# A decoder layer on one core: row scaling moved behind the up product, two beta products shifted, transposes placed later in a planned order

## The chip, the cores and the metric

One core of one Trainium2 chip runs the whole program. Its engines are TensorE (PE in the profile; PEld is its weight load), VectorE (DVE), ScalarE (ACT), GpSimd (POOL) and SyncE (SP), whose queue issues most DMAs. The metric is the device time of one execution in microseconds (us); smaller is better.

## The reference, cut to what matters

Sequence 512, model width 1024, one layer, all in float32. The parts that the change touches are the first projections and the gated MLP:

```
u = rmsnorm(h, g_mix);  proj = u @ w_in            # split into q, k, v, gates, beta and decay inputs (16 columns)
ro = retention(rotary(rq), rotary(rk), rv)          # 8 heads
do = gated_delta(l2norm(cq), l2norm(ck), cv, g, beta)  # 8 heads, chunks of 128, triangular solves
merged = sigmoid(gate_r) * (silu(rgate)*ro @ w_ret_br) + sigmoid(gate_d) * (do*silu(dz) @ w_dn_br)
h = h + merged @ w_o
u2 = (h * rsqrt(mean(h*h) + EPS)) * g_ffn           # one factor for each of the 512 rows
up = causal_dwconv(u2 @ w_up, ffn_conv_w) + ffn_conv_b   # 3 taps along the sequence
a, b = split(up);  h = h + (silu(a) * b) @ w_down
out = rmsnorm(h, g_final)
```

The factor of a row of h can be applied to u2, or to the product u2 @ w_up before the convolution: both give the same numbers up to rounding.

## The kernel before, in words

Each float32 operand of a large product is split in a high part (ACT casts it, `whi`, `ghi`, `u2hi`) and a rest (DVE subtracts, `wlo`, `glo`, `u2lo`), and a product is three matmuls, high by high, high by rest, rest by high (`mm3`, line 387). Weights come in blocks of 128x1024 through `wraw` and are split by the task `weights` (line 351); four split blocks fit (`WB`). The larger square products use seven block products instead of eight (`product`, line 449). Small products and transposes run in plain float32; a transpose is a matmul against the identity `cst`, four at a time (`transpose4`, line 544).

The order of the instructions on PE, ACT, DVE and POOL is the order in which the Python program issues them. A small planner makes it: `Order` (line 98). The long stream of large products is written out in sequence and moves a planned clock on. Everything else is a task, a generator, that waits in a heap until its planned time; `poll` (line 132), called after every three matmuls, lets the tasks run whose time has come. When a task yields, it is put back for the planned end of what it issued, `self.done`, plus 0.3 us, plus what it yields: `yield PW` with `PW = 0.6` (line 282) ahead of a transpose says how much later than the data's planned end the transposes are put into PE's stream. `issue` (line 114) notes the planned end of one instruction; `done` is that of the instruction issued last, also where an earlier one on another engine ends later. The SP queue is not among the engines whose order is set so (line 1795): the framework orders it itself.

The stages, in PE's order:

- Start: 11 warming matmuls, then `first_blocks` (line 1257). For each of the eight k tiles of x, which arrive by DMA and are split as `ghi`, `glo`, it issues three matmuls into `pk`, three into `pq`, and two into `pba` (the 16 beta and decay columns, weights `ba_w`, split by `ba_split`, line 666). The row sums of squares for the first norm go through `pss`.
- Fronts of the delta heads (`k_front`, `q_front`, `v_front`, lines 845 to 940), among products `pk`, `pq`, `pv`, with transposes `pkt`, `pqt`, `pvt`. Between the first four heads and the last four come the retention rows (`pr`), whose rotated rows are transposed (`prqT`, `prkT`, lines 1134 to 1150). `solve` and `scan` (lines 942 to 1078) do the triangular solves and the recurrence (`pm`, `psc`); `scan_end` (line 1080) normalizes a head's rows `vtok` and transposes them (`pot`). Retention's own products are `prs`, `pkv`, `pro`, `proT`.
- Gates (`pz`) and four square products (`py`); at the end of the last, `m_out` (line 1413) transposes the merged rows (`pmt`).
- The product with w_o (`po`) in the order of `OUT_ORDER`. `o_into` (line 1513) adds a result into h (`h`, DVE). When both halves of 128 rows are done it squares them (`junk`, ACT), makes the row factor `rr` (DVE, then a power on POOL, `rsqrt`), multiplies the rows by it into `hs` (one half on ACT, one on DVE), and `u2_out` transposes `hs` into `pt`. `u2_split` makes `u2hi` and `u2lo` of it, with g_ffn as the scale.
- Up product: 44 blocks, `pa` and `pb` in turn. `ffn_conv` (line 1574) reads the bank: ACT makes `acc` from tap 2 and the bias, DVE adds taps 1 and 0 (two multiply-adds of 512 columns). Silu, the product `r`, and sums for the down product follow. POOL meanwhile issues DMAs for sums of w_down's quarters, each after a tiny instruction `tock` that reads `tick` from ACT (`pace`, line 333).
- Down product (`pd`). `into` (line 1659) adds, squares, and at the end scales the two halves of 128 rows, `o` on ACT and `g` on DVE, and sends both out.

Of the kernel before, what the change touches and what calls it, by code (L numbers as in the profile page):

```python
# [11 lines left out]
F32 = mybir.dt.float32  # L12
F32R = mybir.dt.float32r
AF = mybir.ActivationFunctionType
ALU = mybir.AluOpType
# [82 lines left out]
class Order:  # L98
# [15 lines left out]
    def issue(self, engine, us, banks=()):  # L114

        at = self.clock if self.now is None else self.now
        at = max(at, self.free.get(engine, 0.0))
        for b in banks:
            at = max([at, *(t + self.HOP for e, t in self.banks.get(b, {}).items() if e != engine)])
        self.done = self.free[engine] = at + us  # L120
        for b in banks:
            self.banks.setdefault(b, {})[engine] = self.done

    def product(self, us):
        self.clock += us
# [6 lines left out]
    def poll(self):  # L132
        while self.tasks and self.tasks[0][0] <= self.clock:
            at, _, gen = heapq.heappop(self.tasks)
            self.now, self.done = at, None
            try:
                more = next(gen) or 0.0
                at = (at if self.done is None else self.done + self.HOP) + more
                self.n += 1
                heapq.heappush(self.tasks, (at, self.n, gen))  # L140
            except StopIteration:
                pass
            self.now = None

    def hold(self, cond):
        while not cond():
            self.clock = max(self.clock, self.tasks[0][0])
            self.poll()
# [89 lines left out]
def body(nc, tc, ctx, io):  # L238
# [26 lines left out]
    def s4(name, n=4, bufs=16):  # L265
        return mini.tile([P, n], F32, name=name, tag=f"n{n}", bufs=bufs)
# [259 lines left out]
    def row_scale(ssq, out):  # L526
        r = s4("rs", 1)
        vec.scalar_tensor_tensor(r, ssq[:, :1], EPS, ssq[:, 1:], ALU.add, ALU.add)
        yield
        rsqrt(out, r)  # L530
# [364 lines left out]
    def q_front(hd, ps):  # L895
        h = hd["h"]
        gb = row_decay(h) if "G" in have else None
        qT = hd["qT"] = yield from conv_silu(ps, h, f"q{h}")
        yield PW
        pqt = transpose4(qT, "pqt")  # L900
        yield
        ssq = s4("ssqq")
        junk = S("junk")
        for n in range(NT):
            act.activation(junk[:, ck(n)], pqt[:, ck(n)], AF.Square, accum_out=ssq[:, n:n + 1])
        yield
        vec.tensor_scalar(ssq, ssq, EPS, None, ALU.add)
        rq = s4("rq")
        yield
        rsqrt(rq, ssq)  # L910
        yield
        rqs = hd["rqs"] = mini.tile([P, 4], F32, name="rqs", tag="rqs", bufs=10)
        vec.tensor_scalar(rqs, rq, DK_SCALE, None, ALU.mult)
        while "k" not in hd["got"]:
            yield 0.3
        if gb is None:
            gb = row_decay(h)
        pqk = PS("pqk")
        for n in range(NT):
            pe.matmul(pqk[:, ck(n)], hd["kT"][:, ck(n)], qT[:, ck(n)], start=True, stop=True)  # L920
        yield
        hd["attn"] = em.pop(h)
        vec.tensor_tensor(hd["attn"], pqk, hd["attn"], ALU.mult)
        yield 1.5
        vec.tensor_tensor(qT, qT, gb, ALU.mult)
        hd["got"].add("q")

    def v_front(hd, ps):
        vT = yield from conv_silu(ps, 16 + hd["h"], f"v{hd['h']}")
        while "k" not in hd["got"]:  # L930
            yield 0.3
        yield PW
        pvt = transpose4(vT, "pvt")
        yield
        hd["vtok"] = S(f"vtok{hd['h']}")
        for n in range(NT):
            act.activation(hd["vtok"][:, ck(n)], pvt[:, ck(n)], AF.Identity, scale=hd["c1"][:, n:n + 1])
        hd["got"].add("v")
# [141 lines left out]
    def scan_end(hd, o, ssqo):  # L1080
        h = hd["h"]
        ms = s4("mso")
        vec.tensor_scalar(ms, ssqo, 1.0 / P, EPS, ALU.mult, ALU.add)
        r = s4("ro")
        yield
        rsqrt(r, ms)
        yield
        vec.tensor_tensor(v3(o), v3(o), bc(r), ALU.mult)
        hd["got"].add("o")
        yield PW  # L1090
        pt = transpose4(o, "pot")
        yield
        d = S(f"doT{h}")
        act.activation(d, pt, AF.Identity, scale=prm[:, P_DG:P_DG + 1])
        doT[h] = d
# [37 lines left out]

    def rq_front(t, _, ps):
        x = rotary(ps, t, "qrot")
        yield PW
        pt = transpose4(x, "prqT")
        yield
        q = S(f"rqT{t}")
        vec.tensor_tensor(q, pt, qdec, ALU.mult)  # L1140
        rqT[t] = v3(q)

    def rk_front(t, _, ps):
        x = rotary(ps, t, f"krot{t}")
        yield PW
        pt = transpose4(x, "prkT")
        yield
        k = S(f"rkT{t}")
        act.copy(k, pt)
        rkT[t], krot[t] = v3(k), v3(x)  # L1150
# [103 lines left out]

    pba = PS("pba")

    def first_blocks():

        pss = [PS(n) for n in ("pk", "pq")]
        ws = [tuple(v3(a, KT) for a in w) for w in first_w]  # L1260
        for k in range(KT):
            hold(lambda: k in g_ready)
            for i, ps in enumerate(pss):
                hold(lambda: (i, k // 4) in first_ready)
                mm3(ps, ws[i][0][:, k], ws[i][1][:, k], ghi[k], glo[k], k == 0, k == KT - 1)
                poll()
            hold(lambda: "ba" in first_ready)
            for j, x in enumerate(gx):
                pe.matmul(pba[:32], ba_w[:, k], x[k], start=(k + j == 0), stop=(k + j == KT))
            poll()  # L1270
        for i in range(2):
            spawn(weights(), 0.1 + 8.0 * i)
        spawn(decays(pba), 0.2)
        return pss
# [136 lines left out]
        o_opnd[name, t] = hi, lo  # L1411

    def m_out(t, i, r):
        yield 0.2
        pt = transpose4(r, "pmt")
        yield
        name, half = f"B{i + 1}{t // 2 + 1}", t % 2
        m = o_raw[name, half] = S(f"mr{t}{i}")
        act.copy(m, pt)
        yield  # L1420
        if name != "B12":
            spawn(o_split(name, half, m))
        if name == "B12":
            t3 = S("mt3")
            vec.tensor_tensor(t3, o_raw["B22", half], m, ALU.subtract)
            t2 = o_raw["T2", half] = S("mt2")
            vec.scalar_tensor_tensor(t2, t3, -1.0, o_raw["B11", half], ALU.mult, ALU.subtract)
            spawn(o_split("T2", half, t2), 0.2)
            yield 0.5
            t1 = S("mt1")  # L1430
            vec.tensor_tensor(t1, o_raw["B11", half], m, ALU.subtract)
            spawn(o_split("T1", half, t1), 0.2)
            spawn(o_split("T3", half, t3), 0.2)
        elif name == "B21":
            while o_now[0] < 3:
                yield 0.5
            t4 = S("mt4")
            vec.scalar_tensor_tensor(t4, o_raw["T2", half], -1.0, m, ALU.mult, ALU.subtract)
            spawn(o_split("T4", half, t4), 0.2)
# [68 lines left out]

    u2hi = [S(f"u2hi{k}", F32R) for k in range(KT)]
    u2lo = [S(f"u2lo{k}", F32R) for k in range(KT)]  # L1510
    ssqs = [s4("ssq1", 2) for _ in range(NT)]

    def o_into(t, i, ps, op, last=False):

        vec.tensor_tensor(h1[t][i], h1[t][i], ps, op)
        yield
        if not last:
            return
        junk = S("junk")
        act.activation(junk, h1[t][i], AF.Square, scale=1.0 / 32.0, accum_out=ssqs[t][:, i:i + 1])  # L1520
        if i == 0:
            return
        yield
        rr = s4("rr", 1)
        yield from row_scale(ssqs[t], rr)
        yield
        for i2 in range(2):
            xs = S("hs")
            if i2:
                vec.tensor_scalar(xs, h1[t][i2], rr, None, ALU.mult)  # L1530
            else:
                act.activation(xs, h1[t][i2], AF.Identity, scale=rr)
            spawn(u2_out(t, i2, xs), 0.6 * (i2 + 1))

    u2_ready = set()

# [35 lines left out]


    def ffn_conv(ps, ci):
        w = prm[:, P_FW + 3 * ci:P_FW + 3 * ci + 3]
        acc = S2("acc")
        act.activation(acc, ps, AF.Identity, scale=w[:, 2:3], bias=prm[:, P_FB + ci:P_FB + ci + 1])
        yield
        for j in (1, 0):
            s = 2 - j  # L1580
            vec.scalar_tensor_tensor(acc[:, s:], ps[:, :T - s], w[:, j:j + 1], acc[:, s:], ALU.mult, ALU.add)
        yield
        return acc
# [75 lines left out]
    def into(t, i, ps, op, c=slice(0, T), last=False):  # L1659
# [26 lines left out]
        o = hg[t, 1 - i]  # L1686
        act.activation(o, o, AF.Identity, scale=rr)
        vec.tensor_scalar(g, g, rr, None, ALU.mult)
        for k in (1 - i, i):
            sp.dma_start(ov[t, :, ck(k, T)], hg[t, k])  # L1690

    done = [0] * NT
# [106 lines left out]
```

## Time and profile before

| what | value |
|---|---|
| median of 3 runs | 981.6 us (980.06 to 982.82) |
| profiled execution, own time | 980.2 us |
| span from first to last instruction | 978.3 us |
| outside the span | 1.9 us |
| mean granted TensorE clock | 0.999 |
| PE busy | 963.4 us, 98% |
| DVE busy | 748.2 us, 76% |
| ACT busy | 529.1 us, 54% |
| POOL busy | 165.1 us, 17% |

A row of the timeline gives start, duration, engine, line, operation, output<-inputs, shape, and in brackets the engine's idle time before it and who ended it. Matmuls overlap in the profile: what counts is the distance from one start to the next. A float32 matmul stands as two records.

### The profile page before, as it was taken

Reading aid. Unit: us, or ns where it says so; the run is one execution under the profiler, and the core shown is the slowest. Engines: PE = TensorE matmul, PEld = TensorE weight load, DVE = VectorE, ACT = ScalarE, POOL = GpSimd, SP = SyncE. Lnnn points to the kernel's source line nnn. Section 1 sums busy time; section 2 is a strip of 40 time slices with the busy share of each in tenths; the row PEclk is TensorE's granted clock in tenths of the full one; section 3 lists DMA queues with packets and bytes.
Section 4 is the critical chain, followed back from the end, with each engine's and each line's share of the span. In section 5 each row is a group of like instructions: output and inputs, shape, how many; then the busy total and the mean of one; then the engine's idle time right before and its main releaser. Section 6 shows DMA issues by size and latency. Waiting matters only on the chain.

```text
span 978.3 us, 14091 instructions
## 1 busy us (share of the span) xinstructions
PE 963.4 (98%) x5133; PEld 804.6 (82%) x5133; DVE 748.2 (76%) x1359; ACT 529.1 (54%) x1110; POOL 165.1 (17%) x209
## 2 busy tenths in 40 slices
PE   8999999999999999999999999899999999999997
PEld 6888888788888888978888887788888888888886
DVE  6888898567888898585899799865555676688785
ACT  6598222256955323586686646854344434356663
POOL 0121322224344020132000000221122221000001
PEclk9999999999999999999999999999999999999999
DMA  8244569958797695579976855666579998346663
GB/s 277 83 126 143 168 197 215 275 143 214 214 210 215 182 229 147 144 207 270 256 229 197 281 154 160 208 211 217 193 204 213 227 201 195 91 143 191 192 202 118
DMA packets 82949, 189.27 MB, mean 193 GB/s; under 512 B 22912, under 2 KB 31680, under 8 KB 82880
## 3 DMA queue, kind: packets, MB, share of 16 engines
q1 hardware_dynamic: 55360, 123.36, 39.4%
q0 software_dynamic: 27520, 65.02, 29.9%
q8 instruction: 40, 0.66, 0.3%
q14 instruction: 29, 0.24, 0.1%
HBM read 185.17 MB, written 68.19 MB: 259 GB/s over the span
## 4 chain that ended last, share of the span: by engine, by line
PE 85%; DVE 6%; ACT 4%; DMA 2%; issue 2%; POOL 0%; SPq 0%; POOLq 0%; DVEq 0%; ACTq 0%
PE pb L230 12%; PE pa L230 12%; PE py L230 12%; PE pd L230 10%; PE pz L230 9%; PE pr L230 9%; PE pq L230 3%; PE pv L230 3%; PE psc L230 3%; PE pk L230 3%; DVE wlo L200 2%; PE po L230 2%; PE pro L230 1%; ACT whi L200 1%; PE pm L230 1%
## 5 line engine op out<-in xcount | busy, mean ns | idle before, releaser
L200 ACT CAST whi<-wraw 128x1024 fp32r<-128x1024 f32 (+1 forms) x214 | 219.9, 1029 | 184.9 <-PE pr L230 54.2
L200 DVE TENSOR_TENSOR wlo<-wraw,whi 128x1024 fp32r<-128x1024 f32 (+1 forms) x214 | 255.3, 1194 | 63.7 <-ACT whi L200 63.1
L200 POOL TENSOR_SCALAR tock<-tick 128x1 f32<-128x1 f32 x72 | 34.0, 472 | 399.6 <-ACT tick L200 399.6
L200 DVE SCALAR_TENSOR_TENSOR acc<-pb,prm,acc 128x511 f32<-128x511 f32 (+1 forms) x44 | 33.0, 749 | 57.0 <-ACT acc L200 56.2
L230 PE MATMUL pa<-u2lo,whi 128*128 128x512 f32 (+1 forms) x192 | 71.4, 372 | 0.0
L230 PE MATMUL pa<-u2hi,whi 128*128 128x512 f32 (+1 forms) x192 | 71.4, 372 | 0.0
L230 PE MATMUL pa<-u2hi,wlo 128*128 128x512 f32 (+1 forms) x192 | 71.3, 371 | 0.0
L230 PE MATMUL pb<-u2hi,whi 128*128 128x512 f32 (+1 forms) x184 | 70.0, 380 | 0.0
L230 PE MATMUL pb<-u2lo,whi 128*128 128x512 f32 (+1 forms) x184 | 69.9, 380 | 0.0
L230 PE MATMUL pb<-u2hi,wlo 128*128 128x512 f32 (+1 forms) x184 | 69.9, 380 | 0.0
L230 PE MATMUL py<-whi,oh 128*128 128x512 f32 x160 | 62.9, 393 | 0.0
L230 PE MATMUL py<-wlo,oh 128*128 128x512 f32 x160 | 62.3, 390 | 0.0
L230 PE MATMUL py<-whi,ol 128*128 128x512 f32 x160 | 62.3, 389 | 0.0
L230 PE MATMUL pd<-whi,T 128*128 128x512 f32 (+1 forms) x198 | 55.3, 366 | 0.0
L230 PE MATMUL pz<-ghi,whi 128*128 128x512 f32 x128 | 51.4, 402 | 0.0
L230 PE MATMUL pr<-whi,ghi 128*128 128x512 f32 x128 | 51.1, 399 | 0.0
L230 PE MATMUL pr<-whi,glo 128*128 128x512 f32 x128 | 50.0, 390 | 0.0
L230 PE MATMUL pz<-ghi,wlo 128*128 128x512 f32 x128 | 49.9, 390 | 0.0
L230 PE MATMUL pz<-glo,whi 128*128 128x512 f32 x128 | 49.9, 390 | 0.0
L230 PE MATMUL pr<-wlo,ghi 128*128 128x512 f32 x128 | 49.9, 390 | 0.0
L200 DVE SCALAR_TENSOR_TENSOR acc<-pa,prm,acc 128x511 f32<-128x511 f32 (+1 forms) x44 | 33.0, 749 | 19.0 <-ACT acc L200 18.2
L200 ACT ACTIVATE acc<-pb,prm 128x512 f32<-128x512 f32 x22 | 17.2, 780 | 48.5 <-PE pb L230 48.5
(331 smaller groups left out, 2416.2 us busy)
## 6 DMA issues: line engine op xcount, KB each, us to landing
wraw<-w SPq DMA_DIRECT2D x98, 512.0 KB, 4.8
s<-wm POOLq DMA_DIRECT2D x30, 1024.0 KB, 8.2
wraw<-s SPq DMA_DIRECT2D x60, 512.0 KB, 3.8
s<-wd POOLq DMA_DIRECT2D x24, 704.0 KB, 5.5
wraw<-wm SPq DMA_DIRECT2D x30, 512.0 KB, 4.5
s<-s POOLq DMA_DIRECT2D x10, 1024.0 KB, 11.8
wraw<-wd SPq DMA_DIRECT2D x15, 512.0 KB, 3.6
s<-s POOLq DMA_DIRECT2D x8, 704.0 KB, 9.4
```

The lines of the kernel that those rows point to most:

```text
L200: return f(out, *args, **kw)
L230: self.engine.matmul(out, lhsT, rhs, start=start, stop=stop, **kw)
```

## The change

Seven edits in one file:

- `Order.issue`: `done` becomes the latest planned end of all that a task issued since it last yielded, and not that of its last instruction. Every task that issues on two engines between yields can so come back later; this alone shifts places all over the program.
- Transposes are offered later: `q_front`, `v_front`, `rq_front` and `rk_front` yield 1.5 in place of `PW` (0.6); `scan_end` of heads 4 to 7 yields 2.4; `m_out` yields 1.6 in place of 0.2.
- `first_blocks`: the two `pba` matmuls of tile k are issued with tile k+2 (`ba_part`), and the last two pairs behind the loop.
- The second norm: h goes into the transposes unscaled, as soon as its last sum is in. The squares of all eight halves are collected, `o_scales` makes one factor per row, spreads it along the columns by a float32 matmul `pR` of ones by `diag`, and ACT copies it to the tile `R2` (named R in the order).
- `ffn_conv`: DVE first multiplies the bank by that tile into `scaled` (128x512, in SBUF), 44 times, and the three taps then read `scaled` and not the bank.
- `into`: the loop that sends the two halves out runs over (i, 1 - i), not (1 - i, i).

```
-        self.done = self.free[engine] = at + us
+        self.free[engine] = at + us
+        self.done = max(self.done or 0.0, at + us)
...
         qT = hd["qT"] = yield from conv_silu(ps, h, f"q{h}")
-        yield PW
+        yield 1.5
         pqt = transpose4(qT, "pqt")
...
         hd["got"].add("o")
-        yield PW
+        yield PW if h < GH else 2.4
         pt = transpose4(o, "pot")
...
+            if k > 1:
+                ba_part(k - 2)
+        for k in range(KT - 2, KT):
+            ba_part(k)
...
     def m_out(t, i, r):
-        yield 0.2
+        yield 1.6
         pt = transpose4(r, "pmt")
...
+        if last:
+            spawn(u2_out(t, i, h1[t][i]))
+            spawn(o_square(t, i), 2.0)
+
+    def o_square(t, i):
         junk = S("junk")
+        act.activation(junk, h1[t][i], AF.Square, scale=1.0 / 32.0, accum_out=ssq2[:, i, t:t + 1])
+        yield
+        squared.append((t, i))
+        if len(squared) == 2 * NT:
+            yield from o_scales()
+
+    def o_scales():
+
+        ms, rr = s4("ms2"), s4("rr2")
+        vec.scalar_tensor_tensor(ms, ssq2[:, 0], EPS, ssq2[:, 1], ALU.add, ALU.add)
+        yield
+        rsqrt(rr, ms)
+        yield
+        diag = S("diag")
+        vec.tensor_tensor(v3(diag), ident.unsqueeze(1).to_broadcast([P, NT, P]), bc(rr), ALU.mult)
+        yield
+        ps = PS("pR")
+        pe.matmul(ps, ones, diag, start=True, stop=True)
+        yield
+        R = S("R2")
+        act.copy(R, ps)
+        yield
+        scale2.append(R)
...
     def ffn_conv(ps, ci):
+        while not scale2:
+            yield 0.3
         w = prm[:, P_FW + 3 * ci:P_FW + 3 * ci + 3]
+        x = S("scaled")
+        vec.tensor_tensor(x, ps, scale2[0], ALU.mult)
+        yield
+        ps = x
         acc = S2("acc")
...
-        for k in (1 - i, i):
+        for k in (i, 1 - i):
             sp.dma_start(ov[t, :, ck(k, T)], hg[t, k])
```

Three places in the order that this makes. First PE in `first_blocks`: `pk` and `pq` are the large products, `pba` the beta product, the number behind `ghi` and `glo` tells the k tile (141 and 149 are tile 0, 142 and 150 tile 1, 143 and 151 tile 2). Before:

```order
L230 MATMUL pq<-ghi_141,wlo 128x512
L230 MATMUL pba<-ghi_141,ba_w 32x512
L230 MATMUL pba<-glo_149,ba_w 32x512
L230 MATMUL pk<-ghi_142,whi 128x512
L230 MATMUL pk<-glo_150,whi 128x512
```

And now, from the last product of tile 0 on:

```order
L231 MATMUL pq<-ghi_141,wlo 128x512
L231 MATMUL pk<-ghi_142,whi 128x512
L231 MATMUL pk<-glo_150,whi 128x512
L231 MATMUL pk<-ghi_142,wlo 128x512
L231 MATMUL pq<-ghi_142,whi 128x512
L231 MATMUL pq<-glo_150,whi 128x512
L231 MATMUL pq<-ghi_142,wlo 128x512
L231 MATMUL pk<-ghi_143,whi 128x512
```

The two beta products of tile 0 now stand behind tile 2; at the end of the stage six `pba` matmuls stand in a row behind the four `pss<-ones,sq` matmuls, where before there were six products of tile 7 and two `pba`. The order of DVE's first 37 rows, the splits and squares of this stage, is the same.

Second PE at the end of the w_o product, where `po` is that product and `pt` the transposes for u2; `hs` is a scaled half of rows, `h_21` the second half of row block 2 itself. Before, the first `pt` stood in the last product but few:

```order
L230 MATMUL po<-wlo,mT_6325 128x512
L235 MATMUL pt<-cst,hs 128x128 x4
L230 MATMUL po<-whi,mT_6319 128x512
L230 MATMUL po<-whi,mT_6320 128x512
L230 MATMUL po<-wlo,mT_6319 128x512
L235 MATMUL pt<-cst,hs 128x128 x12
L230 MATMUL po<-whi,mT_6319 128x512
```

Now they begin 26 rows earlier:

```order
L231 MATMUL po<-wlo,mB_6271 128x512
L236 MATMUL pt<-cst,h_21_5711 128x128 x4
L236 MATMUL pt<-cst,h_20_5709 128x128 x4
L231 MATMUL po<-whi,mB_6276 128x512
L231 MATMUL po<-whi,mB_6277 128x512
L231 MATMUL po<-wlo,mB_6276 128x512
L236 MATMUL pt<-cst,h_30_5713 128x128 x4
L231 MATMUL po<-whi,mB_6276 128x512
```

Seven of the eight groups of four stand ahead of the first `pa`, where before there were four, and the last stands between the first `pa` and the first `pb`. The matmul `pR` stands behind the ninth product of the fourth half block.

Third DVE in the up product, where `acc` is the convolution, `wlo` a weight block's rest, and `R` the spread row factor. Before, for one pair of blocks:

```order
L200 SCALAR_TENSOR_TENSOR acc<-pa,prm,acc 128x511
L200 SCALAR_TENSOR_TENSOR acc<-pa,prm,acc 128x510
L200 TENSOR_TENSOR wlo<-wraw,whi 128x1024
L200 SCALAR_TENSOR_TENSOR acc<-pb,prm,acc 128x511
L200 SCALAR_TENSOR_TENSOR acc<-pb,prm,acc 128x510
L200 TENSOR_TENSOR wlo<-wraw,whi 128x1024
L200 TENSOR_TENSOR r_7200<-acc 128x512
```

And now:

```order
L201 TENSOR_TENSOR scaled<-pa,R_6676 128x512
L201 TENSOR_TENSOR B_7125<-r_7120,B_7125 128x256
L201 TENSOR_TENSOR wlo<-wraw,whi 128x1024
L201 SCALAR_TENSOR_TENSOR acc<-scaled,prm,acc 128x511
L201 SCALAR_TENSOR_TENSOR acc<-scaled,prm,acc 128x510
L201 TENSOR_TENSOR scaled<-pb,R_6676 128x512
L201 TENSOR_TENSOR wlo<-wraw,whi 128x1024
L201 SCALAR_TENSOR_TENSOR acc<-scaled,prm,acc 128x511
L201 SCALAR_TENSOR_TENSOR acc<-scaled,prm,acc 128x510
L201 TENSOR_TENSOR r_7210<-acc 128x512
```

A multiplication of the whole bank has come in ahead of each pair of multiply-adds, and it is what waits for PE there. Counted in this order, at the n-th `scaled` (n from 4 on) the rests of n+3 up blocks have been made.

On SP, the last two transfers of the program stand in the same order in both programs: first the half that DVE scales, then the one that ACT scales.

More of the change, by code (lines that the diff above doesn't have):

```diff
@@ L119, in issue @@
             at = max([at, *(t + self.HOP for e, t in self.banks.get(b, {}).items() if e != engine)])
-        self.done = self.free[engine] = at + us
+        self.free[engine] = at + us
+        self.done = max(self.done or 0.0, at + us)
         for b in banks:
-            self.banks.setdefault(b, {})[engine] = self.done
+            self.banks.setdefault(b, {})[engine] = at + us
     def product(self, us):
@@ L931, in v_front @@
             yield 0.3
-        yield PW
+        yield 1.5
         pvt = transpose4(vT, "pvt")
@@ L1089, in scan_end @@
         hd["got"].add("o")
-        yield PW
+        yield PW if h < GH else 2.4
         pt = transpose4(o, "pot")
@@ L1135, in rq_front @@
         x = rotary(ps, t, "qrot")
-        yield PW
+        yield 1.5
         pt = transpose4(x, "prqT")
@@ L1144, in rk_front @@
         x = rotary(ps, t, f"krot{t}")
-        yield PW
+        yield 1.5
         pt = transpose4(x, "prkT")
@@ L1255, in body, with ba_part @@
     pba = PS("pba")
+    def ba_part(k):
+        hold(lambda: "ba" in first_ready)
+        for j, x in enumerate(gx):
+            pe.matmul(pba[:32], ba_w[:, k], x[k], start=(k + j == 0), stop=(k + j == KT))
+        poll()
     def first_blocks():
@@ L1266, in first_blocks @@
                 poll()
[L1267 to L1270, printed above, removed]
+            if k > 1:
+                ba_part(k - 2)
+        for k in range(KT - 2, KT):
+            ba_part(k)
         for i in range(2):
@@ L1510, in body @@
     u2lo = [S(f"u2lo{k}", F32R) for k in range(KT)]
-    ssqs = [s4("ssq1", 2) for _ in range(NT)]
+    ssq2 = const.tile([P, 2, NT], F32, name="ssq2")
+    squared = []
+    scale2 = []
     def o_into(t, i, ps, op, last=False):
@@ L1516, in o_into @@
         yield
-        if not last:
-            return
+        if last:
+            spawn(u2_out(t, i, h1[t][i]))
+            spawn(o_square(t, i), 2.0)
+    def o_square(t, i):
         junk = S("junk")
-        act.activation(junk, h1[t][i], AF.Square, scale=1.0 / 32.0, accum_out=ssqs[t][:, i:i + 1])
-        if i == 0:
-            return
+        act.activation(junk, h1[t][i], AF.Square, scale=1.0 / 32.0, accum_out=ssq2[:, i, t:t + 1])
         yield
-        rr = s4("rr", 1)
-        yield from row_scale(ssqs[t], rr)
-        yield
[L1527 to L1533, printed above, removed]
+        squared.append((t, i))
[4 more added lines that the diff above has]
+        vec.scalar_tensor_tensor(ms, ssq2[:, 0], EPS, ssq2[:, 1], ALU.add, ALU.add)
+        yield
+        rsqrt(rr, ms)
[10 more added lines that the diff above has]
+        scale2.append(R)
     u2_ready = set()
```

## The prediction

> **What bounds the kernel now.** I read the page first, then PE's waits, then the timeline around each wait, and last what DVE does in the up product.
>
> ```profile
> span 978.3 us, 14091 instructions
> PE 963.4 (98%) x5133; PEld 804.6 (82%) x5133; DVE 748.2 (76%) x1359; ACT 529.1 (54%) x1110; POOL 165.1 (17%) x209
> ```
>
> PE is the bound from end to end, so the change can win only what PE waits, and lose only what it makes PE wait or compute anew. The waits of PE, from the view of who waited for whom (total, times, longest):
>
> ```profile
> PE pt L235 <- ACT hs L200: 2.0, 2, 1.6
> PE pba L230 <- DVE ba_w L200: 1.7, 1, 1.7
> PE pot L235 <- DVE vtok L200: 1.2, 1, 1.2
> ...
> PE pm L230 <- DVE m L200: 0.8, 1, 0.8
> PE po L230 <- DVE wlo L200: 0.8, 1, 0.8
> PE pt L235 <- DVE hs L200: 0.7, 1, 0.7
> PE pqt L235 <- ACT q L200: 0.4, 1, 0.4
> PE psc L230 <- ACT tt L200: 0.3, 1, 0.3
> ```
>
> The reader sees nine waits that sum to 7.9 us; the change aims at those on pt, pba, pot and pqt, 6.0 us of it. Where nothing is waited for, the chain of waits gives the price of a product:
>
> ```profile
> 660.36 5.44 PE pa L230 x24
> ```
>
> 24 matmuls in 5.44 us are 0.227 each. A wait costs from the start that was due to the start that came, some tenths more than its row in the list, and I use starts below.
>
> **The start.** The timeline of tile 0 and what stands ready for tile 1 and 2, and the end of the stage:
>
> ```profile
> 7.61 0.50 PE L230 MATMUL pq<-ghi,wlo 128*128 128x512 f32 x1
> 7.87 0.72 ACT L200 ACTIVATE ghi<-xt,prm 128x512 fp32r<-128x512 f32 x1 [1.04 <-DMA xt<-xt]
> 8.62 0.75 DVE L200 SCALAR_TENSOR_TENSOR glo<-xt,prm,ghi 128x512 fp32r<-128x512 f32 x1 [1.07 <-ACT ghi L200]
> 9.77 0.42 PE L230 MATMUL pba<-ghi,ba_w 128*32 128x512 f32 x1 [1.65 <-DVE ba_w L200]
> ...
> 20.62 0.69 DVE L200 TENSOR_TENSOR sq<-sq 128x512 f32<-128x512 f32 x1
> ...
> 21.36 0.97 PEld L230 LDWEIGHTS pss<-ones,sq 128*128 128x128 f32 x8 [0.41 <-DVE sq L200]
> ```
>
> Due at 7.84 (7.61 + 0.23), pba started at 9.77: 1.93 us. With pba moved behind tile 2, PE goes on with tile 1, but its high part ends at 8.59 and its rest at 9.37. So by 9.77 PE has done one product at 8.6 and two from 9.4 on, about 0.6 us of work, and 1.3 us of the wait stays, now for x. Even that is not all kept: the pss matmuls wait for the last sum of squares on DVE, whose order here is unchanged and which ends at 21.3. They start at 21.36 again; behind them stand now six pba (1.36 us) where six products and two pba stood (1.82 us). The term is **-0.5 us**; bounds 0 (x lands later) and -1.9 (all of the wait).
>
> **The fronts and scans.** Offering pqt 0.9 us later ends a wait of 0.4 us: **-0.4**. Nobody waits for the queue behind it, since products of the stream take its place. The two solve waits, pm for m (0.8) and psc for tt (0.3), are not aimed at; in the new order retention products pro stand between the two halves of pm, which covers the first. Against that, the new rule for `done` reshuffles the first group's solve and scans, where PE gets its fillers three at a time (0.68 us) between products that wait for ACT and DVE, and such waits can come up anew. I take gain and new waits as equal, **0**, and keep -1.1 and +3 as ends (+3: half a dozen waits of the size of the pm and psc rows).
>
> The second group's end:
>
> ```profile
> 431.23 2.46 POOL L200 TENSOR_TENSOR ro<-mso,mhalf 128x4 f32<-128x4 f32 x2
> ...
> 432.54 0.39 PE L230 MATMUL py<-wlo,oh 128*128 128x512 f32 x1
> 434.08 0.66 PE L235 MATMUL pot<-cst,vtok 128*128 128x128 f32 x4 [1.16 <-DVE vtok L200]
> ```
>
> Due at 432.77, pot came at 434.08: 1.31 us. Offered 1.8 us later, in the new order 24 products (5.4 us) stand between the last psc and the first pot, and 3 to 6 between one pot and the next. Four powers on POOL at 1.23 each are 4.9 us and run beside that. **-1.3**; 0 if the powers come late again.
>
> **From w_o to the up product.** The transposes' starts and what the matmul pR costs by its twin at the start of the program, pss by diag:
>
> ```profile
> 616.45 0.39 PE L230 MATMUL po<-wlo,mT 128*128 128x512 f32 x1
> 617.29 0.66 PE L235 MATMUL pt<-cst,hs 128*128 128x128 f32 x4 [0.45 <-ACT hs L200]
> ...
> 618.48 1.09 PE L235 MATMUL pt<-cst,hs 128*128 128x128 f32 x8
> 620.25 0.66 PE L235 MATMUL pt<-cst,hs 128*128 128x128 f32 x4 [0.68 <-DVE hs L200]
> ```
>
> ```profile
> 626.76 0.28 PE L230 MATMUL pb<-u2hi,wlo 128*128 128x256 f32 x1
> 627.82 0.72 ACT L200 ACTIVATE hs<-h,rr 128x512 f32<-128x512 f32 x1 [1.64 <-POOL rr L200]
> 628.59 1.09 PE L235 MATMUL pt<-cst,hs 128*128 128x128 f32 x8 [1.55 <-ACT hs L200]
> ```
>
> ```profile
> 25.60 1.02 PE L230 MATMUL pss<-diag,ones 128*128 128x512 f32 x2
> 26.06 0.79 PE L230 MATMUL pv<-ghi,whi 128*128 128x512 f32 x1
> 26.69 0.39 PE L230 MATMUL pv<-glo,whi 128*128 128x512 f32 x1
> ```
>
> Lost: 0.61 (due 616.68, came 617.29), 0.88 (eight at 0.11 from 618.48 make 619.37 due, 620.25 came), 1.71 (626.88 due with 0.12 for 256 columns, 628.59 came): 3.2 us. All three are the way sum, square, power on POOL, scaling, transpose. Now the transposes want the sum alone, and the row factor is wanted only by `scaled`. pR costs 26.69 - 25.60 less one product, 0.86. Three more groups of transposes I take at nothing: eight took 1.09 and four 0.66, so one costs 0.11 and the rest, 0.22 a group, is the last one's end, which lies under the next product; if it did not, it were 0.7. So **-3.2 + 0.9 = -2.3**.
>
> Its cover is ACT, which must still make 32 u2hi, 8 squares and some 4 casts here:
>
> ```profile
> 612.74 0.62 ACT L200 ACTIVATE junk<-h 128x512 f32<-128x512 f32 x1
> ...
> 618.76 4.21 ACT L200 ACTIVATE u2hi<-pt,prm 128x128 fp32r<-128x128 f32 x16
> ...
> 624.40 1.16 ACT L200 CAST whi<-wraw 128x1024 fp32r<-128x1024 f32 x1
> ...
> 626.16 1.62 POOL L200 TENSOR_TENSOR rr<-rs,mhalf 128x1 f32<-128x1 f32 x1
> ```
>
> That is 8.4 + 8 x 0.65 + 4 x 1.16 = 18.2 us. PE gives it the time from the first pt to pR: 36 products (8.2), 81 of half width (9.7) and 32 transposes (3.5), 21.4 us. Behind the last square come the sum, POOL's power (up to 1.6) and diag (some 0.7): 2.5 us. 18.2 + 2.5 = 20.7, so pR is ready about when PE comes to it; the bound of this term is a wait of 0 to +1.5.
>
> The w_o product keeps its wait for wlo (0.8): DVE is as full there and its order nearly the same. **0**, ends -0.8 and +1. Placing `pmt` 1.4 us later is in that.
>
> **The up product.** 44 multiplications of a bank by the row factor come onto DVE. The rows that price them, the multiply-adds, and DVE's room:
>
> ```profile
> L200 DVE TENSOR_TENSOR scaled<-pk,R x8: 672/682/691, 28.0 to 299.4; 128x512 f32<-128x512 f32 x8
> L200 DVE SCALAR_TENSOR_TENSOR k<-scaled,prm,k x24: 742/749/1124, 31.0 to 303.3; 128x511 f32<-128x511 f32 x8, 128x510 f32<-128x510 f32 x8, 128x509 f32<-128x509 f32 x8
> ...
> L200 DVE SCALAR_TENSOR_TENSOR acc<-pa,prm,acc 128x511 f32<-128x511 f32 x22 | 16.5, 749 | 18.2 <-ACT acc L200 18.2
> ...
> 640.00:760.00 120.00, 120.00 (x547) 100.02 (x546) 71.80 (x93) 54.89 (x91) 24.06 (x38) 1.00 0.73 209
> 760.00:867.00 107.00, 107.00 (x474) 88.60 (x473) 73.03 (x109) 39.83 (x59) 15.24 (x20) 1.00 0.77 171
> ```
>
> (min/median/max ns in the first two; in the last two PE, PEld, DVE, ACT, POOL busy.) 44 x 0.682 = 30.0 us. The multiply-adds take 749 ns from the bank (acc) as from SBUF (k), so nothing comes back there. In the second half, the fuller one, DVE goes from 73.0 to 73.0 + 20 x 0.682 = 86.6 of 107 us. The work is hidden under PE's stream, which does not wait once here, and by the new order three up blocks stand ready split when `scaled` waits for a block: 3 x 5.44 = 16.3 us of lead. **0.** [...]
>
> **The end.** SP's last two transfers stand in the same order as before, and SP is the engine whose order the program does not set. **0.**
>
> **The sum** is -0.5 - 0.4 - 1.3 - 2.3 = -4.5 us. Against the profiled execution, 980.2 us (span 978.3 and 1.9 around it), that gives 975.7. The median of the runs shown is 981.6, 1.4 above that execution, so the forecast for a median is 981.6 - 4.5 = **977.1 us**. About 0.3%, 2.9 us, is what a measurement of this kernel can tell from no change.
>
> **The rivals.** *The waits come back elsewhere.* The reshuffled solves and scans cost +3 and pR waits 1: 977.1 + 4 = 981.1, no change. For it: that section has the pm and psc waits, and the rule for `done` moves almost every task. Against it: PE waits there only 1.1 us now, and later offers make fewer waits. Chance 0.24.
>
> *DVE becomes the bound of the up product, and the kernel is slower.* The multiply-adds now have both inputs in SBUF; the longest k row took 1124 ns instead of 749. If all 40 of the second half took that, they would add 40 x 0.375 = 15.0, and if its 20 wlo, also SBUF by SBUF, were stretched by half of their 1.2 us, 12 more: 86.6 + 15.0 + 12.0 = 113.6 of 107 us, 6.6 too much. It decides once DVE's work in that half passes 107 us and the lag is carried past the lead into the down product's operands. Then 977.1 + 6.6 = 983.7. Against it: wlo takes 1217 ns in the mean in this stage and was not stretched beside POOL's DMAs:
>
> ```profile
> L200 DVE TENSOR_TENSOR wlo<-wraw,whi 128x1024 fp32r<-128x1024 f32 x43 | 52.3, 1217 | 4.8 <-ACT whi L200 4.8
> ```
>
> Chance 0.06. [...]
>
> *The change does not do what it says* holds for the last transfers and is in the sum.
>
> **How the numbers follow.** The forecast has 0.60, gains larger than 7 us (all of pm, psc and wlo too) 0.04, the waits that come back 0.24, DVE as the bound 0.06, other new waits that outweigh the gain 0.06. Faster by over 0.3%: 0.60 + 0.04 = 0.64; within 0.3%: 0.24; slower: 0.12. The range reaches from -8 (the forecast with its best bounds: 1.1 + 0.8 + 1.4 more) to the case of no change: 973.5 to 981.5; beside that the forecast's own is 974.5 to 979.
>
> **What would show it.** Right: no pt wait over 0.5 us, pot and pqt gone from PE's waits, pba's wait replaced by one of pk for ghi and glo of about 1.3 us, pss near 21.4; `scaled` at about 682 ns x44 in the up product and PE without a wait there; the stretch from the last SP transfer to the end unchanged. Wrong: waits over 3 us in all on psc, pm, pro; a wait of pR over 1.5; any wait of pa or pb on wlo; or a span that falls by more than 8.

## The result, and the profile after

| | before | changed |
|---|---|---|
| first comparison, six runs of each, median | 980.58 us | 973.75 us |
| ratio, 95% interval | | 0.9930, 0.9909 to 0.9951 |
| second comparison, median (11 and 5 runs) | 979.68 us | 974.11 us |
| ratio, 95% interval | | 0.9943, 0.9931 to 0.9955 |
| profiled execution of the first: time, span | 980.2, 978.3 | 973.08, 971.4 |

The kernel became faster by 6.8 us (4.8 to 8.9) in the first comparison and by 5.6 us (4.4 to 6.8) in the second; the forecast was 4.5. Two executions, one with the beta products alone (1203.36 us) and one with the old rule for `done` (1204.55 us), ran at a mean granted clock of 0.75 and are in none of the ratios below. The page of the changed kernel, and all of PE's waits of 0.2 us or more:

```profile
span 971.4 us, 14183 instructions
...
PE 962.6 (99%) x5135; PEld 805.1 (83%) x5135; DVE 775.6 (80%) x1397; ACT 529.7 (55%) x1107; POOL 169.2 (17%) x206
```

```profile
PE pq L231 <- ACT doT L201: 1.8, 1, 1.8
PE warm L231 <- DVE mhalf L201: 1.1, 1, 1.1
```

All waits of the prediction's list (pt, pba, pot, pqt, pm, po, psc) are gone, the last three of which the change did not aim at, and one is new: pq for doT. PE's busy time hardly moved (963.4 to 962.6 us). The chain of waits shows where the time went; the last product of before, then of the changed kernel:

```profile
867.08 100.17 PE pd L230 x453
```

```profile
860.26 100.17 PE pd L231 x453
```

The down product lasts the same 100.17 us, and it starts 6.82 us earlier. So all of the gain lies ahead of it, and nothing was won or lost at the end of the program.

The rows of the changed kernel that answer to those of the pot and pt waits, and the matmul pR (no bracket is behind any of them: none waited):

```profile
426.42 0.60 PE L236 MATMUL pot<-cst,vtok 128*128 128x128 f32 x4
...
606.90 1.20 PE L236 MATMUL pt<-cst,h 128*128 128x128 f32 x8
...
621.35 0.60 PE L236 MATMUL pt<-cst,h 128*128 128x128 f32 x4
...
628.62 1.02 PE L231 MATMUL pR<-diag,ones 128*128 128x512 f32 x2
```

What pR needs, on DVE:

```profile
627.29 0.69 DVE L201 TENSOR_TENSOR diag<-cst,rr 128x512 f32<-128x512 f32 x1 [1.16 <-POOL rr L201]
```

diag ends at 627.98 and PE comes to pR at 628.62: it was ready 0.64 us early. The up product in the same two stretches as before (PE, PEld, DVE, ACT, POOL busy), and its groups:

```profile
640.00:760.00 120.00, 120.00 (x531) 99.38 (x530) 88.45 (x121) 53.88 (x88) 28.94 (x38) 1.00 0.74 212
760.00:867.00 107.00, 107.00 (x474) 88.60 (x473) 85.36 (x130) 45.44 (x66) 17.63 (x18) 1.00 0.71 165
```

```profile
L201 DVE SCALAR_TENSOR_TENSOR acc<-scaled,prm,acc 128x510 f32<-128x510 f32 x44 | 33.0, 750 | 1.5
L201 DVE SCALAR_TENSOR_TENSOR acc<-scaled,prm,acc 128x511 f32<-128x511 f32 x44 | 32.8, 744 | 0.0
...
L201 DVE TENSOR_TENSOR scaled<-pb,R 128x512 f32<-128x512 f32 x22 | 15.2, 690 | 36.3 <-PE pb L231 36.3
L201 DVE TENSOR_TENSOR scaled<-pa,R 128x512 f32<-128x512 f32 x22 | 15.1, 686 | 10.9 <-PE pa L231 10.9
```

PE does not wait in the up product. The 44 multiplications took 30.3 us of DVE (15.2 + 15.1, forecast 30.0), DVE was busy for 85.4 of 107 us in the fuller half (forecast 86.6), and still waited 47 us for PE ahead of `scaled`.

### The profile page after: what moved, and what is told of

It is laid out like the page before. It is cut to its first block, busy times and chain, and to the rows that moved or that the text cites. A ratio compares the mean times of both kernels' runs of the same rounds, so it can differ in the third digit from the quotient of the medians.

```text
span 971.4 us, 14183 instructions
## 1 busy us (share of the span) xinstructions
PE 962.6 (99%) x5135; PEld 805.1 (83%) x5135; DVE 775.6 (80%) x1397; ACT 529.7 (55%) x1107; POOL 169.2 (17%) x206
## 4 chain that ended last, share of the span: by engine, by line
PE 98%; ACT 1%; issue 0%; DVE 0%; POOLq 0%; POOL 0%
PE py L231 16%; PE pa L231 12%; PE pb L231 12%; PE pd L231 10%; PE pz L231 9%; PE pr L231 9%; PE pk L231 5%; PE pq L231 5%; PE pv L231 5%; PE po L231 4%; PE psc L231 3%; PE pro L231 1%; PE pm L231 1%; PE pqk L231 1%; PE pkk L231 1%; PE warm L231 1%
## 5 line engine op out<-in xcount | busy, mean ns | idle before, releaser
L201 POOL TENSOR_SCALAR tock<-tick 128x1 f32<-128x1 f32 x72 | 41.0, 570 | 534.7 <-ACT tick L201 534.7
L201 DVE SCALAR_TENSOR_TENSOR acc<-scaled,prm,acc 128x511 f32<-128x511 f32 x88 | 65.6, 747 | 1.5
L201 DVE TENSOR_TENSOR scaled<-pb,R 128x512 f32<-128x512 f32 x22 | 15.2, 690 | 36.3 <-PE pb L231 36.3
L231 PEld LDWEIGHTS pa<-u2hi,whi 128*128 128x128 f32 x192 | 36.2, 189 | 6.5 <-issue 0.2
```

The lines of the kernel that those rows point to most:

```text
L201: return f(out, *args, **kw)
L231: self.engine.matmul(out, lhsT, rhs, start=start, stop=stop, **kw)
```

## The experiments

The theory is that of the prediction: each edit is worth the waits of PE that it takes away, less those that it makes, and the time follows the sum of PE's waits. Against it stood, for the part of the gain that was not forecast, the rule for `done` as its source; for the start, that the whole wait of pba could be won; and for the end of the gain, DVE's load.

**One edit at a time.** Four kernels, each the kernel before with one edit of the diff above. The beta products alone:

```
+            if k > 1:
+                ba_part(k - 2)
+        for k in range(KT - 2, KT):
+            ba_part(k)
```

> The kernel before with the beta products shifted, and nothing else. Theory 1 (the forecast's working): the start wins 0.5 us, because the sums of squares on DVE end when they did; PE's first pv starts about 0.5 earlier than in before. Rival (the whole wait): tile 1 of x is there when PE comes, DVE's order is the same but it has its squares earlier, and pv starts 1.5 to 1.9 earlier. Both: in the planned order of this kernel the sixteen transposes pot of the first four heads stand in a row, as they do after the change and did not before. If that row is what makes the new wait of pq for doT at 247 us, this kernel has a wait of about 1.8 us there, and the edit by itself wins nothing in the sum (theory 1: -0.5 + 1.9 = 1.4 slower; rival: -1.7 + 1.9 = 0.2 slower, with what the solves and scans win or lose on top). If the wait is the doing of another edit, there is none here, and the kernel is 0.5 or 1.7 us faster.

Measured: ratio 0.9983 (0.9974 to 0.9992), 1.7 us faster (0.8 to 2.5). The start in the timeline, before and here:

```profile
21.36 1.05 PE L230 MATMUL pss<-ones,sq 128*128 128x1 f32 x8
...
24.21 0.39 PE L230 MATMUL pv<-ghi,whi 128*128 128x512 f32 x1
```

```profile
21.21 1.01 PE L230 MATMUL pss<-ones,sq 128*128 128x1 f32 x8
...
23.47 0.39 PE L230 MATMUL pv<-ghi,whi 128*128 128x512 f32 x1
```

From pss to pv it is 2.85 us before and 2.26 here: 0.6 is won, by fewer matmuls behind the sums of squares, and pss itself starts with DVE's last sum as it did. That is theory 1. PE's waits tell the rest:

```profile
PE pt L235 <- ACT hs L200: 2.0, 2, 1.6
...
PE pq L230 <- ACT doT L200: 1.1, 1, 1.1
...
PE po L230 <- DVE wlo L200: 0.8, 1, 0.8
```

The wait for doT is already here, so it belongs to this edit. But pm, the larger wait for psc, and pot are gone as well, 170 to 410 us behind the only lines that were edited. PE's order there is another one: the sixteen pots of the first four heads stand in a row from 245.91 us on, where in before they stand in four groups apart, the last at 247.04. The code that issues them is the same, so it is the planner that placed them elsewhere. That it did so because the plan no longer holds at the start for `ba_w` is argued, not shown; that the edit does it is shown. The wait for doT was expected at 1.8 us; it is 1.24 by starts, with three products of pk behind the row.

The rule for `done` alone (the first hunk of the diff):

> The kernel before with the new rule for done alone: a task comes back for the planned end of the latest of all it issued. Theory 1 (the forecast's working): gain and new waits in the solves and scans are equal, within 1 us of before, and the start, pqt, pot and pt wait as in before. Rival (the rule is where the part of the gain comes from that was not forecast): the waits of pm for m, psc for tt and po for wlo, 2.4 us by starts, go here already, and the kernel is about 2 us faster.

Measured: ratio 1.0010 (0.9999 to 1.0021), 1.0 us slower (0.1 faster to 2.1 slower). Its waits:

```profile
PE pt L236 <- ACT hs L201: 3.1, 3, 1.6
PE pot L236 <- DVE vtok L201: 1.4, 1, 1.4
...
PE pot L236 <- ACT doT L201: 1.0, 1, 1.0
PE po L231 <- DVE wlo L201: 0.8, 1, 0.8
```

pm and psc go here too, but one more pt wait (1.25 by starts) and one of pot for doT (1.20) come. The rival falls: po still waits for wlo, the kernel is not 2 us faster, and so the rule is not where the unforecast gain comes from.

The six later offers alone (`yield PW` to 1.5 or 2.4, 0.2 to 1.6):

> The kernel before with the six later offers alone (pqt, pvt, prqT, prkT, the second group's pot, pmt). Theory 1 (the forecast's working): the waits of pqt (0.4 to 0.5) and pot (1.3) go, 1.7 us faster; pm, psc and wlo wait as before. Rival: moving the transposes of the retention rows and of v takes away the waits of pm and psc as well, 3.2 us faster. Second rival: a later offer only moves the wait to those behind it, and the kernel is within 0.5 us of before.

Measured: ratio 0.9970 (0.9959 to 0.9982), 2.9 us faster (1.8 to 4.0). Its waits:

```profile
PE pt L235 <- ACT hs L200: 2.0, 2, 1.5
...
PE pm L230 <- DVE m L200: 0.8, 1, 0.8
...
PE psc L230 <- ACT tt L200: 0.3, 1, 0.3
PE pkt L235 <- ACT k L200: 0.3, 1, 0.3
```

pqt and pot are gone, pm and psc stay, as theory 1 had it; a wait of pkt of the size of pqt's has come. What it did not have: po no longer waits for wlo. Of the four edits this alone removes that wait, so 0.9 us of the gain are the offers', most likely pmt's, the only one near; that, and how it does it, is not shown.

The second norm alone (`o_into` to `o_scales`, and `ffn_conv`):

> The kernel before with the second norm moved behind the up product, and nothing else. Theory 1 (the forecast's working): the three waits of pt go (3.2 us by starts), pR costs 0.9, the 44 multiplications on DVE are hidden: 2.3 us faster, and the wait of po for wlo at 603.6 (0.9) stays. Rival: pt's waits were shared with a general lag of ACT and DVE in this stage, and with the scaling gone the wait for wlo goes too: 3.2 us faster. A second rival, that the multiplications cost something in the up product: the stretch from the first pa to the last pb is longer than in before by more than pR's 0.9 us, and the gain is under 1.5.

Measured: ratio 0.9973 (0.9964 to 0.9982), 2.6 us faster (1.8 to 3.5). The first four of its waits:

```profile
PE pot L235 <- DVE vtok L200: 1.1, 1, 1.1
PE warm L230 <- DVE mhalf L200: 1.1, 1, 1.1
PE pm L230 <- DVE m L200: 0.8, 1, 0.8
PE po L230 <- DVE wlo L200: 0.8, 1, 0.8
```

No pt, wlo as before, no wait in the up product: theory 1, 2.3 forecast.

**The new wait.** What stands around it on PE, and on ACT, in the changed kernel:

```profile
245.13 1.97 PE L236 MATMUL pot<-cst,vtok 128*128 128x128 f32 x16
248.87 0.50 PE L231 MATMUL pq<-ghi,whi 128*128 128x512 f32 x1 [1.77 <-ACT doT L201]
```

```profile
243.31 2.47 ACT L201 ACTIVATE gb<-gb,nG 128x128 f32<-128x128 f32 x8
245.80 1.28 ACT L201 ACT_TABLE_LOAD   x1
247.09 1.15 ACT L201 ACTIVATE gb<-gb 128x512 f32<-128x512 f32 x2
248.15 1.83 ACT L201 ACTIVATE doT<-pot,prm 128x512 f32<-128x512 f32 x3
```

Four heads' pots stand in a row, each in a bank of PSUM of its own; the program has eight. The copies that free them stand in ACT's queue behind eight gb, a table load and two gb. pq reads nothing that doT makes: it waits for a bank. Of the kernels that follow, the first takes back the rule for `done` in the changed kernel:

> The changed kernel with the old rule for done (done is that of the instruction issued last). By itself that rule made before slower by 1.0 us (0.1 faster to 2.1 slower). Theory 1 (the parts add): without it the changed kernel is about 1 us faster. Theory 2 (the rule's loss came with waits of pt for hs and of pot for doT, and the first of these, 1.25 us, cannot come in a kernel whose transposes read h): within 0.3 us of the changed kernel. Both: the sixteen pots still stand in a row, and pq waits about 1.8 us for doT.

Measured: ratio to before 0.9938 (0.9925 to 0.9951), 6.1 us faster than before, between the changed kernel's two results. The interval (4.8 to 7.4) holds theory 1's 1 us as well, so the times alone do not decide. The waits do: behind the start there is the one of pq for doT, 1.8 us as forecast, as in the changed kernel, and none of pt or pot. That is theory 2: the rule's loss came with waits that no longer come here.

The others offer the pots of the first four heads later (`yield PW if h < GH else 2.4` becomes `yield 2.4`, and 8.0 or 4.0 for the first four):

> The changed kernel with the transposes pot of the first four heads offered 1.8 us later, as those of the last four are. In the planned order two pots then stand ahead of pq and the other two behind three and four products of it. Theory 1 (the wait is for a bank of PSUM: four pots hold four of the eight, and none comes free until ACT has made the first doT, at 248.87): pq does not wait, but the third pot takes a bank that doT must free, comes about 0.7 us later and waits then; of the 1.9 us at most 0.7 goes. Rival (the row of sixteen itself is the trouble, and spread out it costs nothing): the wait goes, 1.9 us faster.

Measured: ratio to before 0.9929 (0.9917 to 0.9940), 7.0 us faster than before. The fourth pot in the timeline:

```profile
249.54 0.66 PE L236 MATMUL pot<-cst,vtok 128*128 128x128 f32 x4 [0.80 <-ACT doT L201]
```

It is the fourth that waits, not the third as expected, 0.97 by starts in place of 1.93: a little more than expected went, and the wait did not. It is the same place in the count: in the changed kernel pq, and here the fourth pot, is the fifth to ask for a bank, and starts when the first doT has ended (248.15 + 0.67 there, 248.81 + 0.67 here). Spreading the row out is not enough.

> The changed kernel with the transposes pot of the first four heads offered 7.4 us later, behind eleven products of pq, so that ACT has its table loaded and its queue worked off when they come. Theory 1 (a bank of PSUM, and ACT's lag behind): no wait at 247 us, 1.9 us faster than the changed kernel, with nothing late in its place. Rival: ACT is the one that is late, and the next in want of it (pv, pqk) waits instead; the gain is under 0.7 us.

Measured: the profiled execution took 971.38 us and has no wait at this place; the five others took 974.49 to 977.28, ratio 0.9953 (0.9937 to 0.9969). Profile and times disagree, so both this kernel and one between the two were run beside the changed kernel:

> The changed kernel once more, on the chip of the next three, so that they can be compared with it. All theories: 6 to 8 us faster than before, with the one wait of pq for doT; the first pv between 22.6 and 23.5, as the first tiles of x land.

Measured: 974.11 us (973.75 to 975.72), the second row of the table at the head. In this execution the sums of squares started as late as in before (21.41 against 21.36), so that the two can be compared wait by wait; pv started at 23.71, 0.50 earlier than in before, and the gain was 5.6 us, both just outside what was expected. The down product here:

```profile
861.76 100.17 PE pd L231 x453
```

5.32 earlier than in before.

> The kernel whose first four pots are offered 7.4 us later, once more: its profiled execution took 971.38 and had no wait at 247 us, the timed ones 974.49 to 977.28 at clocks of 0.995 to 0.999. Theory 1 (those executions lost their time to the granted clock and not to the order): the median is 971.5 to 972.5 wherever the clock is 0.998 or more, and executions at 0.995 to 0.997 are 2 to 5 us longer, since 0.004 of 965 us are 3.9. Rival (the order itself is worth less): the median is again above 974 at clocks of 0.998 or more.

Measured: 971.58 us median, ratio 0.9929 (0.9910 to 0.9948). Four executions at clocks of 0.998 to 1.000 took 970.97 to 971.82, two at 0.997 took 975.71 and 975.89: theory 1 in that the order is worth what the profile said. That the clock is the whole reason of the longer ones is not shown: 0.001 to 0.003 of 970 us are 1 to 3 us, and they took some 4 more. One execution of the earlier run, 974.49 at 0.999, is not explained by it at all.

> The changed kernel with the transposes pot of the first four heads offered 3.4 us later: two pots ahead of pq, nine products, the third pot, three products, the fourth. Theory (a bank of PSUM): the third pot is due at about 246.0 + 0.9 + 2.05 = 248.9, when the first doT has just ended; no wait over 0.3 us, 1.6 to 1.9 us faster than the changed kernel. Rival (the stage has no room, and whatever comes off one wait comes back in another, as the offer 7.4 us later seems to show with its 975.95): within 0.7 us of the changed kernel or slower.

Measured: 971.99 us (971.51 to 972.21), ratio to before 0.9918 (0.9905 to 0.9930), 2.1 us below the changed kernel beside it. The third and fourth pot, after nine products and three more, with the first doT on ACT:

```profile
248.83 0.67 ACT L201 ACTIVATE doT<-pot,prm 128x512 f32<-128x512 f32 x1
248.84 0.60 PE L236 MATMUL pot<-cst,vtok 128*128 128x128 f32 x4
...
249.97 0.60 PE L236 MATMUL pot<-cst,vtok 128*128 128x128 f32 x4
```

Neither waits. The third starts together with the first doT, and not behind its end as was expected, so it still found a bank free; the fourth, the fifth to ask, comes at 249.97, after the first doT has ended at 249.50. Held back until ACT has come to the copies, the pots cost nothing; this version beats both kernels.

**DVE's cover.** Each bank is multiplied again, into a tile that nothing reads, two and three more times:

```
+        for _ in range(2):
+            y = S("again")
+            vec.tensor_tensor(y, ps, scale2[0], ALU.mult)
         yield
```

> The changed kernel with the multiplication of each bank done three times, twice into a tile that nothing reads: 88 more instructions of 0.682 us, 60 us, on DVE in the up product. Theory 1 (DVE's room is the cover, and it ends at full): the second half would need 86.6 + 40 x 0.682 = 113.9 of 107 us, so DVE is full, PE waits for wlo or a bank, and the kernel is 5 to 10 us slower. Rival (planning puts splits first and lets the convolutions lag, and the lead and the down product's first operands take it up): under 2 us slower.

Measured: 973.93 us (973.54 to 975.08), ratio to before 0.9941 (0.9928 to 0.9954): as fast as the changed kernel, within what can be told. The two stretches, and the idle time ahead of `scaled` (last column):

```profile
640.00:760.00 120.00, 120.00 (x531) 99.38 (x530) 113.79 (x166) 54.29 (x90) 28.81 (x40) 1.00 0.77 213
760.00:867.00 107.00, 107.00 (x473) 88.59 (x472) 105.40 (x167) 43.90 (x64) 14.01 (x17) 1.00 0.72 163
```

```profile
L201 DVE TENSOR_TENSOR scaled<-pa,R 128x512 f32<-128x512 f32 x22 | 15.1, 688 | 3.1 <-PE pa L231 3.1
L201 DVE TENSOR_TENSOR scaled<-pb,R 128x512 f32<-128x512 f32 x22 | 15.1, 685 | 2.6 <-PE pb L231 2.6
```

DVE is busy 98% of the second half, the idle time ahead of `scaled` has gone from 47.2 us to 5.7, and PE still does not wait. Theory 1 was wrong for this load, and a piece of DVE's timeline shows why:

```profile
801.26 0.69 DVE L201 TENSOR_TENSOR scaled<-pa,R 128x512 f32<-128x512 f32 x1
801.87 1.28 DVE L201 TENSOR_TENSOR again<-pa,R 128x512 f32<-128x512 f32 x2
803.06 0.68 DVE L201 TENSOR_TENSOR r<-acc 128x512 f32<-128x512 f32 x1
...
812.14 0.69 DVE L201 TENSOR_TENSOR scaled<-pa,R 128x512 f32<-128x512 f32 x1
```

From start to start a multiplication in a queue takes 0.60 us (two from 801.87 to 803.06), not the 0.68 of its record: an instruction starts before the one ahead has ended. Priced so, the 88 are 53 us and not 60. And the next `scaled` of a pa comes 10.88 us later, which is just PE's time for a pair of blocks (2 x 5.44): DVE is full, and keeps pace. The rival's number, under 2 us, held, and some of its lag is there: the last multiply-add starts at 868.4, 7.7 us behind the last start of pb, where in the changed kernel it is 863.1 and 3.3.

> The changed kernel with the multiplication of each bank done four times, three of them into a tile that nothing reads: 132 more instructions of 0.68 us, 90 us. With three multiplications DVE was busy for 113.8 of 120 and 105.4 of 107 us, with 5.7 us of idle time before scaled left, and PE did not wait. Theory 1 (the cover ends when DVE has no idle time left): 90 us on 47 us of idle time in the stage (36.3 + 10.9) is 43 us too much; less a lead of 16 the kernel is 15 to 30 us slower, and PE waits for wlo or for a bank. Rival (the lag is carried into the down product, whose stage leaves DVE 26 us): under 8 us slower.

Measured: 985.94 us, ratio to before 1.0068 (1.0054 to 1.0083), 11.8 us above the changed kernel beside it. PE's waits on `wlo`, and the ten us in which the longest wait of pb ends:

```profile
PE pd L231 <- DVE wlo L201: 4.1, 3, 2.5
PE pb L231 <- DVE wlo L201: 3.6, 4, 1.8
```

```profile
860.00:870.00 10.00, 9.23 (x34) 7.47 (x35) 9.93 (x15) 3.29 (x6) 0.00 (x0) 0.83 0.37 120
```

Here the splits wlo are late, from 823 us on, and PE waits 7.7 us for them; the clock of 0.83 in the quoted ten us comes on top (0.17 of ten us, an estimate of 1.7 us). The last multiply-add starts 21 us behind the last start of pb. A fourth multiplication brings DVE's pair of blocks to some 12.0 us (10.88 and two more of 0.60), 1.2 above PE's. Over 22 pairs that is 26 us, less the lead of 16 makes 10; 11.8 was measured. That is reckoned behind the result: the expectations were 15 to 30, by the full durations, and under 8.

**The sum.** PE's waits of 0.2 us or more behind the start, counted from the start due to the start that came and with pR at 0.86, against the measured times (sums worked out before rounding; a minus is faster):

| kernel | waits | start, pss to pv | both, against before | measured against before |
|---|---|---|---|---|
| before | 7.6 | 2.85 | | |
| beta products | 6.2 | 2.26 | -2.1 | -1.7 (-2.5 to -0.8) |
| `done` | 8.5 | 2.85 | +0.9 | +1.0 (-0.1 to 2.1) |
| offers | 5.1 | 2.85 | -2.6 | -2.9 (-4.0 to -1.8) |
| second norm | 5.0 | 2.75 | -2.7 | -2.6 (-3.5 to -1.8) |
| changed, profile of the first comparison | 2.8 | 2.31 | -5.4 | -6.8 (-8.9 to -4.8) |
| changed, profile of the second | 3.0 | 2.30 | -5.2 | -5.6 (-6.8 to -4.4) |
| changed, old rule for `done` | 2.8 | 2.21 | -5.5 | -6.1 (-7.4 to -4.8) |
| pots 2.4 | 1.8 | 2.20 | -6.4 | -7.0 (-8.1 to -5.9) |
| pots 4.0 | 0.9 | 2.21 | -7.4 | -8.0 (-9.3 to -6.9) |
| pots 8.0, first run | 0.9 | 2.31 | -7.3 | -4.6 (-6.2 to -3.0) |
| pots 8.0, second run | 0.9 | 2.21 | -7.4 | -7.0 (-8.8 to -5.1) |
| three multiplications | 2.8 | 2.32 | -5.4 | -5.8 (-7.1 to -4.5) |
| four multiplications | 11.6 | 2.20 | +3.3 | +6.7 (+5.3 to +8.1) |

Every row but two agrees within its interval: the time is PE's stream plus what PE waits. The two are the first run of pots 8.0, whose profiled execution alone came to -8.6 and whose other five are only in part explained, and the four multiplications, where the clock of 0.83 adds 1.7 us by that estimate and leaves the sum still 0.3 short of the interval. The edits do not add up one by one, since pm, psc and pot are each taken away by more than one of them.

## Why the prediction was right, and where it was not

The sign and the way were right: PE's waits go, and the time follows. The gain was larger than the 4.5 us forecast, by 2.3 in the first comparison and by 1.1 in the second. The medians, 973.75 and 974.11, lie under the forecast's own 974.5 to 979 and inside the whole range; 1.0 and 1.9 us of that come from before, whose median here was 980.58 and 979.68 and not 981.6. By its steps:

- **Start, -0.5: right.** 0.50 with x landing alike, 0.6 from pss to pv. That the first profile won 1.6 (pv at 22.64) was the landing of x: among the ten profiles with the shifted products pss started anywhere from 20.33 to 21.41. The fourth tile of x landed at 9.09 us there, at 10.17 in the second profile and at 10.11 in before, and pss started 11.2 us later each time. The wait of 1.3 us for x in the place of pba's was not there in the first profile; with the old rule for `done` it was 1.2 (0.65 for ghi, 0.56 for glo by starts), in the second profile of the changed kernel 0.5.
- **pqt, -0.4, and pot, -1.3: right**, shown by the offers alone; there a wait of pkt came in place of pqt's, in the changed kernel none.
- **Fronts and scans, 0: the step that failed, in its terms though not in its balance.** "I take gain and new waits as equal" held: 1.46 (pm and psc) went and 1.93 (doT) came. But the gain and the loss were put down to the rule for `done`, and the beta products alone bring both; the rule alone takes pm and psc away too, and brings a wait for doT of its own (1.20). The new wait is not of the kind that was bounded, a product that waits for data, but a wait for a bank behind ACT's queue, and the planned order of the changed kernel, which has the four pots in a row, could have shown it.
- **From w_o to up, -2.3: right**, 2.6 (1.8 to 3.5) alone. The margin of pR was 0.64 us.
- **The wait of po for wlo, 0: wrong in size.** The end of its bounds, -0.8, was the answer (0.93 by starts); the later offers took it away. This and the start are why the first comparison's profiled execution came out above the forecast; where x landed in its other executions is not known.
- **Up product, 0: right**, and with more room than the reckoning by durations gave: DVE could take twice the added work again (three multiplications: 973.93 us). The multiply-adds took 744 to 750 ns from `scaled` against 749 from the bank. Of the 88 `acc` rows of the changed kernel 24 ran beside POOL's `tock`, which reads one column of SBUF, and no `acc` row took over 753 ns. Ahead of the up product there are longer rows: those of k and v over 1000 ns (three in the changed kernel, 1128 at most) all ran beside POOL's `gb<-gb`, each of 1.1 to 1.6 us.
- **End, 0: right**, the down product and what follows it are unchanged.

The rivals: waits did come back elsewhere, one of 1.9 us, but more went. DVE as the bound did show, but between three multiplications of a bank (973.93 us) and four (985.94), not at one, and the stretched rows by which the rival priced it did not come (in the changed kernel's up product no `acc` row over 753 ns, no `wlo` row over 1226).

## What to carry to other kernels

Where one engine is busy 98% of the time, list its waits and price each from start to start: here a change of order was worth the waits that went less those that came, within the interval in eleven of thirteen rows. An edit at the head of a planned program can remove waits hundreds of us away (170 to 410 here) and make others: read the order at every place where the trace has a wait or where copies queue up, not only at the places that the edit aims at. Four heads' transposes in a row held a PSUM bank each here until ACT had come to their copies, and pq waited 1.8 us for the first; offered 3.4 us later they cost no wait (971.99 us against 974.11), so offer transposes by the queue of the engine that copies them and not by their own data.

## What the runs showed of the hardware

DVE's records overlap: in the kernel with three multiplications 0.68 us of duration are 0.60 from start to start where work is queued, and with DVE busy for 105.40 of 107 us (98%) PE lost nothing there. Other lengths in its timeline from 800 to 822 us overlap by the same 0.08 (0.42 to 0.34 for `y<-r`, 1.22 to 1.14 for `wlo`); from a multiply-add to the next one, which reads its `acc`, it is 0.78 with a record of 0.75, no overlap. A pair of blocks there sums to 11.9 us of durations and took 10.88, so that a sum of durations overstates this full DVE by about a tenth. The granted clock was lower behind one wait and not behind others: behind pb's of 1.8 us with four multiplications it was 0.83 for the ten us quoted; behind pq's of 1.8 us for doT in the changed kernel (250 to 270 us) and behind pd's of 2.5 us with four multiplications (870 to 890 us) it was 1.00, so the length of one wait does not decide it, and what does is not shown. Single executions with a mean granted clock of 0.997 in place of 0.998 to 1.000 took some 4 us longer with the same program in pots 8.0, and 1.1 to 2.0 in the second comparison of the changed kernel. The mean clock does not price the time: one execution with four multiplications took 986.22 us at 0.947, beside 985.38 to 985.66 at 0.996 and 0.997.
